# Rounding and splitting weights: gate and up halves made ahead of each product, down halves made once by the first block

## The chip, the cores and the metric

The kernel runs on one core of a Trainium2 chip. Five engines each work through an instruction stream of their own, strictly in order: TensorE (PE, matrix products), VectorE (DVE), ScalarE (ACT), GpSimd (POOL) and SyncE (SP, which here issues the transfers between DRAM and the on-chip memory). They wait for each other through semaphores. The metric is the time of one execution in device microseconds (us); lower is better.

## The reference

One layer of a hybrid decoder for 2048 prompt rows and 32 sample rows: a mixer (attention and a spatial gate) and then a SwiGLU block, all in float32. The change lies in the SwiGLU block and its weights alone:

```
D_MODEL = 1024
D_FF = 2816

def _swiglu(x, g, w_gate, w_up, w_down):
    h = _rmsnorm(x, g)
    return (jax.nn.silu(h @ w_gate) * (h @ w_up)) @ w_down

x = x + jnp.concatenate([att, u * gate], axis=-1) @ w_out
x = x + _swiglu(x, norm2_g, w_gate, w_up, w_down)
```

## The kernel before

**Precision.** PE multiplies rounded float32 values ("f32r"). To keep float32 accuracy every operand is split into a high part (the value rounded, made by a copy on ACT) and a low part (value minus high part, a subtraction on DVE or POOL). A product of two operands is then three matmuls: high by high, high by low and low by high. In `product` these are lines 1681, 1682 and 1683, and line 1683 is the one that reads the low part of the weights.

**Blocks and steps.** The SwiGLU block runs over three blocks of rows: the first and the second have six tiles of 128 rows, the third has four tiles and the sample rows. Each block runs over f = 0 to 21, the slices of 128 hidden columns. For one f the gate and up products are done with a scheme of seven products in place of eight (q = 0 to 6) on sums and differences of quarters of the weights; `one(u, q)` is one such step, and `product` issues its 12 matmuls (four values of k, three matmuls each). The outputs go to four PSUM banks in turn (`ps_m`), and after each product ACT or DVE takes them out (lines 1693 to 1719).

**Gate and up weights.** The first block loads the quarters (`load_quarter`), multiplies them with the norm's gain on ACT (`gained`, line 1575, four instructions of 128x128 for a quarter), forms the sums on POOL (`sums`, lines 1587 to 1596), stores the seven operands of each f to DRAM (`keep`, tensor `ab_d`), and splits them itself. The second and third block load the seven operands from `ab_d` (`load_source`, a ring of eight `fr` tiles) and split them: the high part by `high` (ACT, line 1603), the low part by `low_half` (POOL, line 1607), into a ring of five `op` tiles. `prepare` does this after the product of a step: behind product q of f it issues the low part of operand q + 3, the high part of operand q + 4 and the load of operand q + 4 of the next f.

**Down weights, first block.** `load_down` brings 128 rows of `w_down` for an even f into `rows2[1]` (tile `fe`) and for an odd f into `rows2[0]` (tile `fd`); `split_down` splits them (ACT line 136, POOL line 139, 128x1024) into tiles `dw`. The down products (`down_unit`, line 1961) follow steps 3, 4 and 5 of each even f, two tiles of rows each, in two PSUM banks (`ps_o`), and DVE adds each result to the row sums `acc` (line 1963). `block_sums` forms four differences of down weights for the later blocks on DVE (line 1652 at step 2 of an odd f, lines 1654 to 1656 at step 0 of the next even f) and stores them to `td_d` at step 4 of the odd f and step 2 of the even f.

**Down weights, second and third block.** Class `Seven` uses the seven-product scheme for the down products as well, on a pair of f (an odd f and the even one before it) and on pairs of row tiles. It needs seven weight operands d = 0 to 6 for a pair of f, an eighth (7) for the sample rows in the third block. Operands 2, 3, 4 and 6 come from `td_d`, operands 0, 1, 5 and 7 are halves of `w_down`; they are loaded at steps 1, 2 and 4 of the odd f (`load`), and `split` makes both parts (ACT line 1810; DVE or POOL line 1811) at steps 2 to 6 of the odd f and steps 0 and 2 of the even f. The hidden values get their own sums and splits (`even`, `odd_a`, `odd_b`, `odd_c`, `put`: lines 1815, 1816, 1850 to 1863). From step 3 of the even f on, `woven` puts one down product (three matmuls, line 1898) behind each k of the gate and up products until none is left: 21 for a pair in the second block; 14, and 4 of two matmuls for the sample rows, in the third. DVE adds each to `acc` (line 1900). Between step 1 of the odd f and step 2 of the even f there are no down products.

**Order.** Every engine's stream is in the order of the program text. `later(n, ...)` puts work n steps off, and `tick()`, called at the head of `one`, issues what is due. All these transfers go through SP, in order; SP waits where a tile isn't free or data isn't ready.

**Rings that matter here.** `zn_tile` gives one of three tiles of 128x512; in the first block an f uses two of them (the sums at steps 0 and 3). `rows2` are two single tiles. `roll` copies a piece of 512 KB of the caches in DRAM, once per f in the first block, three times in the second and twice in the third.

## Time and profile before

| | us |
|---|---|
| median of three runs | 2735.92 (2733.41 to 2742.21) |
| the profiled execution, its own time | 2734.9 |
| span of its instructions | 2733.1 |

| engine | busy us | share of the span | instructions |
|---|---|---|---|
| PE | 2496.4 | 91% | 13448 |
| DVE | 1772.7 | 65% | 3275 |
| POOL | 1457.0 | 53% | 1138 |
| ACT | 1286.2 | 47% | 2744 |

The SwiGLU block of the three row blocks lies at about 1017 to 1513 us, 1602 to 2139 us and 2216 to 2700 us of the span. In the views, a row of the timeline has the start in us, the duration in us, the engine, the line, the operation, output<-inputs, the shape, the count of instructions merged into the row, and in brackets how long the engine sat idle before it and what released it. A row of a group has the line, engine, operation, tiles, shapes and count, then busy us and mean ns of one, then idle time before it and its releasers. A row of a table by stretches has, for each engine, busy us and the number of instructions, then the granted PE clock (1.00 is full), the share of time in which the 16 DMA engines were busy, and GB/s.

### The profile page before, as it was taken

What the parts mean: (1) busy time and instruction counts of PE and PEld (TensorE: products, weight loads), DVE (VectorE), ACT (ScalarE), POOL (GpSimd) and SP (SyncE); (2) the same over time, 40 slices, a digit from 0 to 9 for tenths busy, and PEclk for the clock granted to TensorE, in tenths of its full rate; (3) what the DMA queues carried; (4) which work ended last, traced back from release to release, by engine and by line L of the source; (5) the groups of instructions that cost most, each with busy time, mean ns of one, the idle gap of its engine ahead of it and who ended that gap; (6) DMA issues with size and microseconds to landing.
All of it is one profiled execution on the core that took longest, in us unless ns stands there. A gap on an engine that the chain in (4) does not pass through costs nothing.

```text
span 2733.1 us, 39993 instructions
## 1 busy us (share of the span) xinstructions
PE 2496.4 (91%) x13448; PEld 2194.9 (80%) x13448; DVE 1772.7 (65%) x3275; ACT 1286.2 (47%) x2744; POOL 1457.0 (53%) x1138
## 2 busy tenths in 40 slices
PE   8998899999999889999999999999989998888886
PEld 6776777778888778999999888888878787777775
DVE  3268784438888775555555667777677756676666
ACT  5423344447777555545454463233342453333343
POOL 1035743234677457868686346455464445555553
PEclk9999999999999999999999999999999998898988
DMA  8764844677777655565655735555555645555553
GB/s 241 217 202 154 284 139 139 200 251 220 233 223 198 188 167 189 188 204 186 207 183 176 240 123 181 166 181 177 166 169 177 195 139 173 178 169 183 164 189 102
DMA packets 335307, 509.98 MB, mean 187 GB/s; under 512 B 28273, under 2 KB 181266, under 8 KB 329214
## 3 DMA queue, kind: packets, MB, share of 16 engines
q1 hardware_dynamic: 329628, 498.37, 57.8%
q10 hardware_dynamic: 5474, 9.04, 1.2%
q8 instruction: 108, 1.77, 0.3%
q14 instruction: 97, 0.79, 0.1%
HBM read 401.11 MB, written 176.32 MB: 211 GB/s over the span
## 4 chain that ended last, share of the span: by engine, by line
PE 32%; issue 11%; POOL 9%; DMA 5%; DVE 4%; ACT 2%; SPq 0%; POOLq 0%; ACTq 0%; DVEq 0%
POOL op L1607 7%; PE ps_m L1683 6%; PE ps_o L1961 6%; PE ps_m L1682 6%; PE ps_m L1681 6%; PE ps_o L1898 5%; DMA fd<-in_w_down_dram 3%; DMA fr<-ab_d 1%; DMA db<-td_d 1%; POOL db L1811 0%; DVE acc L1963 0%; POOL op L1811 0%; PE ps_o L1413 0%; PE ps_o L1415 0%; PE ps_o L1414 0%
## 5 line engine op out<-in xcount | busy, mean ns | idle before, releaser
L1683 PE MATMUL ps_m<-xh,op 128*128 128x384 f32 (+5 forms) x1932 | 638.8, 331 | 125.4 <-POOL op L1607 125.3
L1607 POOL TENSOR_TENSOR op<-fr,op 128x512 fp32r<-128x512 f32 x385 | 524.2, 1378 | 311.5 <-ACT op L1603 307.6
L1681 PE MATMUL ps_m<-xh,op 128*128 128x384 f32 (+5 forms) x1932 | 628.0, 325 | 0.3 <-DVE raw L1711 0.3
L1682 PE MATMUL ps_m<-xl,op 128*128 128x384 f32 (+5 forms) x1932 | 628.2, 325 | 0.0
L1683 PEld LDWEIGHTS ps_m<-xh,op 128*128 128x128 f32 x1932 | 381.8, 198 | 142.0 <-POOL op L1607 140.8
L1681 PEld LDWEIGHTS ps_m<-xh,op 128*128 128x128 f32 x1932 | 381.4, 197 | 21.5 <-issue 0.6
L1682 PEld LDWEIGHTS ps_m<-xl,op 128*128 128x128 f32 x1932 | 380.9, 197 | 17.8
L1900 DVE TENSOR_TENSOR acc<-acc,ps_o 128x512 f32<-128x512 f32 x350 | 239.7, 687 | 127.8 <-PE ps_o L1898 123.8
L1730 ACT ACTIVATE ps_t<-zn 128x384 f32<-128x384 f32 (+1 forms) x126 | 58.6, 465 | 507.6 <-DVE zn L1713 360.3
L1603 ACT ACTIVATE op<-fr 128x512 fp32r<-128x512 f32 x396 | 237.4, 619 | 43.9 <-PE ps_m L1683 37.0
L1961 PE MATMUL ps_o<-dw,hw 128*128 128x512 f32 x840 | 199.3, 392 | 5.5 <-DVE acc L1963 5.5
L319 PE MATMUL ps_s<-wh,xh 128*128 128x512 f32 x480 | 197.4, 411 | 7.3 <-ACT xh L136 6.1
L320 PE MATMUL ps_s<-wl,xh 128*128 128x512 f32 x480 | 191.4, 399 | 0.0
L321 PE MATMUL ps_s<-wh,xl 128*128 128x512 f32 x480 | 191.0, 398 | 0.0
L1961 PEld LDWEIGHTS ps_o<-dw,hw 128*128 128x128 f32 x840 | 156.6, 188 | 40.2 <-DVE acc L1963 8.8
L1963 DVE TENSOR_TENSOR acc<-acc,ps_o 128x512 f32<-128x512 f32 x142 | 96.7, 686 | 80.8 <-PE ps_o L1961 80.8
L1607 POOL TENSOR_TENSOR op<-pair,op 128x512 fp32r<-128x512 f32 x63 | 86.2, 1376 | 97.9 <-ACT op L1603 52.9
L1898 PE MATMUL ps_o<-op,ao 128*128 128x512 f32 x450 | 133.1, 406 | 0.0
L319 PEld LDWEIGHTS ps_s<-wh,xh 128*128 128x128 f32 x480 | 92.4, 192 | 37.1 <-issue 8.4
L321 PEld LDWEIGHTS ps_s<-wh,xl 128*128 128x128 f32 x480 | 92.3, 192 | 20.7 <-DVE xl L139 0.2
L320 PEld LDWEIGHTS ps_s<-wl,xh 128*128 128x128 f32 x480 | 92.8, 193 | 17.7 <-DVE wl L227 0.5
L612 POOL TENSOR_TENSOR vl<-kv,vh 100x512 fp32r<-100x512 f32 (+1 forms) x32 | 45.9, 1438 | 109.3 <-PE ps_t L622 37.0
(548 smaller groups left out, 5789.3 us busy)
## 6 DMA issues: line engine op xcount, KB each, us to landing
fr<-ab_d SPq DMA_DIRECT2D x308, 256.0 KB
out_ks_dram<-in_cache_k_dram SPq DMA_DIRECT2D x56, 512.0 KB
out_vs_dram<-in_cache_v_dram SPq DMA_DIRECT2D x56, 512.0 KB
ab_d<-fr SPq DMA_DIRECT2D x88, 256.0 KB
raw<-in_w_in_dram SPq DMA_DIRECT2D x72, 256.0 KB
fd<-in_w_down_dram SPq DMA_DIRECT2D x70, 256.0 KB
qk_d<-pair SPq DMA_DIRECT2D x64, 256.0 KB
ab_d<-pair SPq DMA_DIRECT2D x63, 256.0 KB
```

Of the source, the lines that this page charges most:

```text
L319: pe.matmul(o[j], xh[:, k, :], wh, start=(k == 0), stop=False)
L320: pe.matmul(o[j], xh[:, k, :], wl, start=False, stop=False)
L321: pe.matmul(o[j], xl[:, k, :], wh, start=False, stop=(k == KD - 1))
L1603: act.activation(ops[f, j][0], ab[f][j], AF.Copy)
L1607: (pool if f or j in POOL_LOW else dve).tensor_sub(lo_, ab[f][j], hi.bitcast(F32))
L1681: pe.matmul(out, wh[:, ks], xh[:, :, k], start=(k == 0), stop=False)
L1682: pe.matmul(out, wh[:, ks], xl[:, :, k], start=False, stop=False)
L1683: pe.matmul(out, wl[:, ks], xh[:, :, k], start=False, stop=(k == 3))
L1898: pe.matmul(ps, l_, r_, start=(new and x == 0), stop=(x == 2), skip_group_check=True)
L1900: dve.tensor_add(acc, acc, ps)
L1961: pe.matmul(ps[0:nr], l_, r_[:, cs], start=(z == 0 and y == 0), stop=(z == FC - 1 and y == len(pairs) - 1))
L1963: dve.tensor_add(B.acc[i][0:nr, cs], B.acc[i][0:nr, cs], ps[0:nr])
```

## The change

Two things change. **Gate and up weights:** in the second and third block, `one` now issues at its head, ahead of `tick()` and of product q, both the high and the low part of operand q + 4 (of operand q - 3 of the next f for q over 2) and the load that follows; `prepare` no longer does this after the product. **Down weights:** the first block now also makes the high part (`block_high`, ACT) and the low part (`block_low`, DVE, in place) of its four differences and stores both parts (`block_keep`, `td_d` is twice as large), and stores both parts of its split down weights (`down_keep`, new tensor `bd_d`). Its sums at step 0 of the even f move to step 5 of the odd f before; the steps of all this stand in the table `FIRST_DOWNS`, whose key is (f % 2, q). `load_down` of an even f moves from step 4 to step 3. In the second and third block `split`, `raw` and `source` are gone: `load` brings both parts of an operand with one transfer of 512 KB straight to where the products read it, operands 0 and 1 at step 1 of the odd f, 2 to 6 at steps 2 to 6, 7 at step 0 of the even f.

```diff
--- before.py
+++ after.py
@@ -118,7 +118,8 @@
     cs_d = dram.tile([SR, D], F32, name="cs_d")
     zs_d = dram.tile([3, SR, DA], F32, name="zs_d")
     ab_d = dram.tile([NF, 7, P, 512], F32, name="ab_d")
-    td_d = dram.tile([NF // 2 - 1, 4, P, 512], F32, name="td_d")
+    td_d = dram.tile([NF // 2 - 1, 4, P, 2, 512], F32, name="td_d")
+    bd_d = dram.tile([NF - 2, P, 2, D], F32, name="bd_d")
 
     ident = consts.tile([P, P], F32, name="ident")
     make_identity(nc, ident)
@@ -1645,20 +1646,54 @@
         raws["d", f] = w_ = rows2[0 if seven else 1 - f % FC]
         sync.dma_start(w_, A["w_down"][f * P:(f + 1) * P, :])
 
-    def block_sums(g, part):
+    def block_sum(g, first):
 
         (t1, t3), (t4, t2) = ((r_[:, 0:512], r_[:, 512:1024]) for r_ in (rows2[1], rows2[0]))
-        if part == 0:
+        if first:
             dve.tensor_sub(t1, t3, t1)
-        elif part == 1:
-            dve.tensor_sub(t3, t2, t3)
-            dve.tensor_sub(t2, t2, t1)
-            dve.tensor_sub(t4, t4, t2)
-        elif part == 2:
-            sync.dma_start(td_d[g, 0], t1)
-        else:
-            for j, t_ in ((1, t2), (2, t3), (3, t4)):
-                sync.dma_start(td_d[g, j], t_)
+            return
+        dve.tensor_sub(t3, t2, t3)
+        dve.tensor_sub(t2, t2, t1)
+        dve.tensor_sub(t4, t4, t2)
+
+    tops = {}
+
+    def block_high(j):
+        t_ = rows2[(1, 0, 1, 0)[j]]
+        src = t_[:, 0:512] if j in (0, 3) else t_[:, 512:1024]
+        hi = zn_tile()
+        act.activation(hi.bitcast(F32R), src, AF.Copy)
+        tops[j] = hi, src
+
+    def block_low(j):
+        hi, src = tops[j]
+        dve.tensor_sub(src.bitcast(F32R), src, hi)
+
+    def block_keep(g, j):
+        for z, x in enumerate(tops.pop(j)):
+            sync.dma_start(td_d[g, j, :, z], x)
+
+    def down_keep(f):
+        for z, x in enumerate(wd[f % FC]):
+            sync.dma_start(bd_d[f, :, z], x.bitcast(F32))
+
+    FIRST_DOWNS = {(1, 2): ((block_sum, True), (down_keep, -1)), (1, 3): ((block_high, 0),),
+                   (1, 5): ((block_sum, False), (block_low, 0)), (1, 6): ((block_keep, 0), (down_keep, 0), (block_high, 2)),
+                   (0, 0): ((block_low, 2),), (0, 1): ((block_keep, 2), (block_high, 1)), (0, 2): ((block_low, 1),),
+                   (0, 3): ((block_keep, 1), (block_high, 3)), (0, 4): ((block_low, 3),), (0, 5): ((block_keep, 3),)}
+
+    def first_downs_ahead(f, q):
+
+        g = f // 2 if f % 2 else f // 2 - 1
+        if not 0 <= g < NF // 2 - 1:
+            return
+        for fn, x in FIRST_DOWNS.get((f % 2, q), ()):
+            if fn is block_keep or fn is block_sum:
+                fn(g, x)
+            elif fn is down_keep:
+                fn(f + x)
+            else:
+                fn(x)
 
     wd = {}
 
@@ -1779,36 +1814,22 @@
             for key in ("s1", "s4"):
                 t_ = pair_tile().rearrange("p a b -> p (a b)")
                 self.a[key] = (self.flat(t_, 0), self.flat(t_, 384))
-            x = [op_tile(True) for _ in range(3)]
+            self.whole = [pool_["fg"].tile([P, 2, 512], F32R, name="op", tag="ox", bufs=3) for _ in range(3)]
             for _ in range(2):
                 t_ = ob_pair("db")
-                x += [(t_[z][:, 0:512], t_[z][:, 512:1024]) for z in range(2)]
+                self.whole += [x.rearrange("p (z c) -> p z c", z=2) for x in t_]
             if self.B.last:
-                x.append((self.B.spare[:, 0:512], self.B.spare[:, 512:1024]))
-            self.d = x
-
-        def source(self, g, d):
+                self.whole.append(self.B.spare.rearrange("p (z c) -> p z c", z=2))
+            self.d = [(x[:, 0], x[:, 1]) for x in self.whole]
+
+        def load(self, g, d):
             j = (None, None, 1, 0, 2, None, 3, None)[d]
             if j is not None:
-                return td_d[g, j]
-            f, half = {0: (0, 0), 1: (1, 0), 5: (1, 1), 7: (0, 1)}[d]
-            f += 2 * g
-            return A["w_down"][f * P:(f + 1) * P, half * 512:(half + 1) * 512]
-
-        def raw(self, d):
-            if d in (0, 1, 5, 7):
-                return rows2[0][:, 0:512] if d in (0, 5) else rows2[0][:, 512:1024]
-            return self.d[d][1].bitcast(F32)
-
-        def load(self, g, *ds):
-            for d in ds:
-                sync.dma_start(self.raw(d), self.source(g, d))
-
-        def split(self, eng, *ds):
-            for d in ds:
-                hi, lo_ = self.d[d]
-                act.activation(hi, self.raw(d), AF.Copy)
-                eng.tensor_sub(lo_, self.raw(d), hi.bitcast(F32))
+                src = td_d[g, j]
+            else:
+                f, half = {0: (0, 0), 1: (1, 0), 5: (1, 1), 7: (0, 1)}[d]
+                src = bd_d[2 * g + f][:, :, half * 512:(half + 1) * 512]
+            sync.dma_start(self.whole[d].bitcast(F32), src)
 
         def put(self, key, src, eng):
             hi, lo_ = self.a[key]
@@ -1930,16 +1951,11 @@
                     self.later_places()
                 if q in (2, 3):
                     self.even(q - 2)
-                if q in (1, 2, 4):
-                    self.load(g, *{1: (0, 1, 2, 3), 2: (4, 6), 4: (5, 7) if self.B.last else (5,)}[q])
-                for eng, ds in {2: ((dve, (0,)), (pool, (1,))), 3: ((dve, (2,)),), 4: ((pool, (3,)),),
-                                5: ((dve, (4,)),), 6: ((pool, (5,)),)}.get(q, ()):
-                    self.split(eng, *ds)
+                for d in ((), (0, 1), (2,), (3,), (4,), (5,), (6,))[q]:
+                    self.load(g, d)
             elif f % 2 == 0 and f:
-                if q == 0:
-                    self.split(pool, 6)
-                if q == 2 and self.B.last:
-                    self.split(pool, 7)
+                if q == 0 and self.B.last:
+                    self.load(g - 1, 7)
                 if f + 2 == NF and q == 3:
                     load_down(f)
 
@@ -2242,6 +2258,15 @@
 
         def one(u, q):
             f = u["f"]
+            if st and u["b"] == B.nt:
+                if f and q < 3:
+                    both_halves(f, q + 4)
+                    if f + 1 < NF:
+                        load_source(f + 1, q + 4)
+                if f + 1 < NF and q > 2:
+                    both_halves(f + 1, q - 3)
+                    if f + 2 < NF:
+                        load_source(f + 2, q - 3)
             tick()
             if st and f and f % 2 == 0 and q == 3:
                 st.begin(f // 2 - 1)
@@ -2253,12 +2278,7 @@
                     sources(B, 2, q, q + 1)
                 return
 
-            if st:
-                if f and q < 5:
-                    prepare(B, f, 4 + q)
-                if f + 1 < NF and q > 2:
-                    prepare(B, f + 1, q - 3)
-            else:
+            if not st:
                 if f and q < 2:
                     prepare(B, f, 7 + q)
                 if f + 1 < NF:
@@ -2283,20 +2303,17 @@
 
             if st and f + 2 < NF:
                 return
-            g = f // 2
             if f % 2 == 0:
-                if q == 4 and 0 < f and not st:
+                if q == 3 and 0 < f and not st:
+                    first_downs_ahead(f, q)
                     load_down(f)
                 if q == 6:
                     split_down(f)
                     load_down(f + 1)
-                if q in (0, 2) and 0 < f and not st:
-                    block_sums(g - 1, 1 + q)
-            else:
-                if q == 3:
-                    split_down(f)
-                if q in (2, 4) and f + 1 < NF and not st:
-                    block_sums(g, q - 2)
+            elif q == 3:
+                split_down(f)
+            if not st and (f % 2 or q != 3):
+                first_downs_ahead(f, q)
 
         def downs_of(pair, a, b):
             for i in rows[a:b]:
```

## The prediction

> **What bounds the kernel now.** I read the groups of the page first, then stretches of the span, then the timeline of PE around one pair of f in each block. PE is busy for 91% of the span, so a gain has to come from its idle time. One group holds nearly all of that in the SwiGLU blocks: the third matmul of a step, the one that needs the low part of a gate or up weight, has waited 125.3 us for POOL's subtraction. In the table by stretches the first block (first row) has PE busy without a gap at full clock, though DVE, ACT and POOL have 44, 50 and 27% of their time free; the second and third block (next two rows) have PE idle and the clock at 0.98 and 0.88. The last row is one stretch without down products in the third block.
>
> ```profile
> span 2733.1 us, 39993 instructions
> ...
> L1683 PE MATMUL ps_m<-xh,op 128*128 128x384 f32 (+5 forms) x1932 | 638.8, 331 | 125.4 <-POOL op L1607 125.3
> ```
>
> ```profile
> core 0: us, PE busy (x) PEld busy (x) DVE busy (x) ACT busy (x) POOL busy (x), PEclk, DMA share, GB/s
> 1097.00:1507.00 410.00, 410.00 (x2158) 383.61 (x2157) 228.09 (x342) 204.68 (x506) 299.18 (x214) 1.00 0.58 190
> 1645.00:2085.00 440.00, 404.00 (x2033) 366.81 (x2034) 313.08 (x491) 148.97 (x296) 230.96 (x167) 0.98 0.53 172
> 2257.00:2660.00 403.00, 333.04 (x1943) 305.29 (x1942) 269.48 (x524) 153.00 (x349) 232.09 (x180) 0.88 0.54 175
> 2418.40:2437.20 18.80, 14.64 (x99) 14.43 (x98) 10.82 (x25) 9.24 (x22) 10.60 (x8) 0.82 0.71 238
> ```
>
> How much is it in all? The wait costs its idle time, and the matmuls behind it run at a lower clock. Both are in the length of a pair of f. The timeline of PE gives it from the same wait at step 2 of f = 2 and, nine pairs later, of f = 20; the other rows are starts of steps of k where nothing waits.
>
> ```profile
> 1645.55 0.69 PE L1683 MATMUL ps_m<-xh,op 128*128 128x384 f32 x1 [2.08 <-POOL op L1607]
> ...
> 2095.95 0.65 PE L1683 MATMUL ps_m<-xh,op 128*128 128x384 f32 x1 [2.59 <-POOL op L1607]
> ...
> 2260.72 0.59 PE L1683 MATMUL ps_m<-xh,op 128*128 128x272 f32 x1 [3.54 <-POOL op L1607]
> ...
> 2666.09 0.60 PE L1683 MATMUL ps_m<-xh,op 128*128 128x272 f32 x1 [3.22 <-POOL op L1607]
> ```
>
> ```profile
> 1653.80 0.34 PE L1681 MATMUL ps_m<-xh,op 128*128 128x384 f32 x1
> ...
> 1656.25 0.34 PE L1681 MATMUL ps_m<-xh,op 128*128 128x384 f32 x1
> ...
> 1678.56 0.33 PE L1681 MATMUL ps_m<-xh,op 128*128 128x384 f32 x1
> ...
> 1680.64 0.33 PE L1681 MATMUL ps_m<-xh,op 128*128 128x384 f32 x1
> ...
> 2403.62 0.29 PE L1681 MATMUL ps_m<-xh,op 128*128 128x272 f32 x1
> ...
> 2407.90 0.29 PE L1681 MATMUL ps_m<-xh,op 128*128 128x272 f32 x1
> ...
> 2419.96 0.29 PE L1681 MATMUL ps_m<-xh,op 128*128 128x272 f32 x1
> ...
> 2424.49 0.29 PE L1681 MATMUL ps_m<-xh,op 128*128 128x272 f32 x1
> ```
>
> Second block: a pair takes (2095.95 - 1645.55) / 9 = 50.0 us. Its 56 steps of k would take, without a wait, 21 with a down product at (1656.25 - 1653.80) / 2 = 1.22 and 35 bare ones at (1680.64 - 1678.56) / 4 = 0.52: 43.9 us. Third block: a pair takes 405.37 / 9 = 45.0 us; 14 steps with a down product at (2407.90 - 2403.62) / 4 = 1.07, 38 bare ones at (2424.49 - 2419.96) / 12 = 0.38, and 4 with two sample matmuls, put at 0.38 + 2/3 of 0.69 = 0.84, make 32.7 us. The excess is 6.1 and 12.3 us per pair.
>
> Why POOL is late is seen on ACT, at the same place in every pair: ACT stands before the high part of a down weight until its transfer has landed, the high parts of the gate and up weights queue behind it, and POOL, which then has both kinds of subtraction to do, starts 4.39 us late.
>
> ```profile
> 2423.98 0.63 ACT L1810 ACTIVATE op<-fd 128x512 fp32r<-128x512 f32 x1 [1.10 <-DMA fd<-in_w_down_dram]
> 2425.64 0.63 ACT L1810 ACTIVATE op<-fd 128x512 fp32r<-128x512 f32 x1 [1.02 <-DMA fd<-in_w_down_dram]
> 2426.17 0.61 ACT L1603 ACTIVATE op<-fr 128x512 fp32r<-128x512 f32 x1
> ```
>
> ```profile
> 2426.34 1.26 POOL L1811 TENSOR_TENSOR op<-fd,op 128x512 fp32r<-128x512 f32 x1 [4.39 <-ACT op L1810]
> ```
>
> **Second and third block: what goes.** All `split` work goes: per pair seven or eight ACT copies with their waits for transfers, three DVE and four or five POOL subtractions. The groups of the third block (2257 to 2660 us of the span) price POOL; the last row is a split of a hidden sum, which stays and is used under the rivals.
>
> ```profile
> L1607 POOL TENSOR_TENSOR op<-fr,op 128x512 fp32r<-128x512 f32 x126 | 168.5, 1355 | 98.4 <-ACT op L1603 98.4
> ...
> L1811 POOL TENSOR_TENSOR db<-db 128x512 fp32r<-128x512 f32 x18 | 24.6, 1364 | 0.0
> ...
> L1811 POOL TENSOR_TENSOR op<-fd,op 128x512 fp32r<-128x512 f32 x9 | 11.4, 1266 | 43.3 <-ACT op L1810 43.3
> ...
> L1816 DVE TENSOR_TENSOR pair<-fe,pair 128x256 fp32r<-128x256 f32 x9 | 13.5, 1496 | 0.0
> ```
>
> From step 1 of the odd f to step 2 of the even f there are nine bare products, 9 x 1.51 = 13.6 us in the third block. POOL has nine low parts there, 9 x 1.36 = 12.2 us, and before the change four or five of the others, about 6 us: 18 us for 13.6, and so a wait. Without them it fits. The ring of five `op` tiles lets operand q + 5 be rounded once product q has ended; 0.61 + 1.36 = 2.0 us later it is ready, and it is needed four products (6.0 us) after. ACT still stands at the SiLU and at the hidden values' splits, 2 to 3 us each, inside that lead. Issuing both halves ahead of the product, rather than the low part a step later, adds lead that the tile ring mostly takes away again; I give it nothing of its own.
>
> I therefore take the whole excess for 9.5 pairs (f = 1 to 19 and half of the last pair, whose own down weights are split as before): 9.5 x (6.1 + 12.3) = 175 us.
>
> **What comes in: transfers.** Each down operand doubles to 512 KB. In the third block the bare stretch then asks for nine loads of 0.26 MB, eight of 0.52 MB and three cache pieces of 0.52 MB, 8.1 MB. The bare stretch of the table moved 238 GB/s at a DMA share of 0.71, so about 335 GB/s is full: 24 us for 13.6. Up to operand 6 (step 6 of the odd f) 6.3 MB are ahead, 19 us; it is needed after the stretch, step 3 (4.3 us) and 2.5 us of step 4, 20.4 us from the start. That is just in time; between 0 and 4 us late per pair I take 1.5, nearer the lower end because the rate above is from a stretch with the same mix. Ten pairs: 15 us. The second block has a stretch of 19.4 us, 27 us until operand 6, and 6.8 MB (20 us) ahead of it: nothing. Left is 175 - 15 = 160 us.
>
> **First block: what it pays.** PE has no gap there, so nothing can be won, and every wait is new. Per pair: four ACT copies (0.61 each), four DVE subtractions, three of the sums moved from the even f's step 0 to the odd f's step 5, and 3 MB of stores more. Averaged, all fits in the free time. The order does not. These rows show the place where it is tight, f = 9 to 10 (step 5 of the odd f ends at 1237.5, step 2 of the even f at 1245.6):
>
> ```profile
> 1237.50 0.55 DVE L1713 TENSOR_TENSOR zn<-zn,ps_m 128x384 f32<-128x384 f32 x1 [0.94 <-PE ps_m L1683]
> ...
> 1240.17 0.57 DVE L1738 TENSOR_TENSOR ps_t<-ps_t,raw 128x384 f32<-128x384 f32 x1
> ...
> 1242.82 1.50 DVE L1654 TENSOR_TENSOR fe<-fd,fe 128x512 f32<-128x512 f32 x1
> 1244.42 1.62 DVE L1655 TENSOR_TENSOR fd<-fd,fe 128x512 f32<-128x512 f32 x1
> 1246.07 0.69 DVE L1656 TENSOR_TENSOR fd<-fd 128x512 f32<-128x512 f32 x1
> ...
> 1247.90 0.55 DVE L1707 TENSOR_TENSOR zn<-raw,ps_m 128x384 f32<-128x384 f32 x1
> 1249.29 0.69 DVE L1963 TENSOR_TENSOR acc<-acc,ps_o 128x512 f32<-128x512 f32 x1 [0.84 <-PE ps_o L1961]
> ```
>
> ```profile
> 1241.38 0.84 ACT L1742 ACTIVATE hw<-ps_t 128x384 fp32r<-128x384 f32 x2
> ...
> 1243.09 2.44 ACT L1575 ACTIVATE fr<-fr,g2c 128x128 f32<-128x128 f32 x8
> 1245.44 0.47 ACT L1693 ACTIVATE zn<-ps_m 128x384 f32<-128x384 f32 x1
> ```
>
> ```profile
> 1237.62 2.41 POOL L139 TENSOR_TENSOR dw<-fd,dw 128x1024 fp32r<-128x1024 f32 x1
> ```
>
> ```profile
> 1247.70 5.64 PE L1961 MATMUL ps_o<-dw,hw 128*128 128x512 f32 x24
> ```
>
> DVE's four subtractions of two on-chip operands take 0.69 to 1.6 us, the more the busier POOL is. After the change DVE starts the three sums at 1238.05; the second writes where POOL's split still reads until 1240.03, so it ends near 1241.7, the third at 1243, `block_low(0)` at 1244.6. Queued behind on DVE are the hidden values of step 6 (lines 1738, 1719, 1738: three times 0.57, until 1246.3, before the change 1240.7). For them wait ACT's two copies of line 1742, and behind those on ACT one high part, the eight gains (2.44 us), `block_high(2)` and the taking out of the even f's product 0 (line 1693): near 1250.7, was 1245.9. Behind it on DVE come `block_low(2)`, lines 1695 and 1697, `block_low(1)` and line 1707, which ends near 1254 (was 1248.45). Only then can DVE add the first down product. PE begins these at 1247.7 and has two banks of six matmuls, 5.64 / 24 x 6 = 1.4 us each, so from about 1250.5 it waits until 1254.7: 4.3 us. SP, too, stands at `block_keep(0)` until 1244.6, and behind it the loads of the next quarters, which ACT wants at step 3 and, itself late, just about gets. Line 1707 also needs a `zn` tile that `block_high(2)` used and that is stored by then, behind some 2.75 MB on SP's queue: at 335 GB/s from 1246 on that is 1254.5, landing a little later. I put the wait at 5.5 us, and 2 us for the lower clock after it, as in the third block, where a pair loses 12.3 us. Bounds: 1 us if POOL leaves DVE alone (four at 0.69), 11 if both the stores and the sums are slow. Ten pairs: 75 us, 10 to 110.
>
> **Sum.** 2734.9 (this execution's own time; 1.0 under the median) - 160 + 75 = 2650 us.
>
> The clock has a rule against part of this. In the second block waits of 2.08 and 2.59 us come with a clock of 0.98. The Trainium skill, page "TensorE: Matmul & The Clock Gate", section "HAM oscillation — how this bites in real kernels", gives "no PE-idle gaps >~3.4µs" as the rule; by it those waits would cost no clock, and their removal would win some 19 us less there (estimate of mine, by that page). The measured 0.98 decides against it here.
>
> **Rivals.** (a) The first block hides its new work: POOL idles in it for 27% of the time, DVE's sums start 5 us earlier, the lead of PE's operands is long. Against: DVE's line 1707 had 1.3 us to spare and gets three subtractions and an ACT queue ahead. Then 2734.9 - 160 + 0 to 20, about 2585. (b) Half of the gain is eaten where POOL no longer waits: DVE's splits of the hidden sums, up to 1.5 us each, have three bare products (4.5 us) without the wait that gave them time, or operand 6 lands late. For: DVE is busy for 67% of the third block (269 of 403 us). Against: the sums are wanted only by the down products of step 3, one k after the other. With a quarter to a half eaten, 2734.9 - 120 + 75 = 2690 to 2734.9 - 80 + 75 = 2730. (c) Slower: the stores in the first block. The `zn` tile of `block_high(2)` comes free only when its store lands, behind 3 MB; at the 190 GB/s that this block moves on average, and not 335, that is 16 us, landing at 1262 to 1264, and DVE and then PE stand until then. It decides from 16 us per pair, where it equals the 160; at 20 us the time is 2734.9 - 160 + 200 = 2775. Against it: 190 goes with a share of 0.58. (d) No change: the low parts are as late as before for a cause that I do not see, and the first block hides its part: 2735.
>
> **How the numbers follow.** Forecast 0.62, (a) 0.16, (b) 0.11, (c) 0.08, (d) 0.03. Predicted is the forecast's 2650. The forecast's own bounds are 2734.9 - 160 + 10 = 2585 and, with operand 6 late by 3 us a pair, 2734.9 - 145 + 110 = 2700. The range 2575 to 2715 holds these, (a) and the better part of (b). A run of this kernel can tell 0.3% (8 us) from no change. Faster holds the forecast, (a) and nearly all of (b): 0.88; slower is (c): 0.08; the same: 0.04.
>
> **What would show it.** In the second and third block no line 1810 or 1811, the wait of line 1683 for POOL under 20 us, pairs of 44 and 33 to 35 us, clock near 1.00. In the first block a new wait of line 1961 for DVE's line 1963 of 4 to 7 us in each even f, pairs of 53 us in place of 45.7, and dips of the clock. I am wrong if the first block stays without gaps, if pairs of the third stay over 38 us, or if PE there waits for DVE or a transfer.

## The result, and where the time went

The changed kernel takes 2663.8 us (median of 4 runs, 2657.6 to 2667.0) against 2738.1 for the kernel before on the same chips (4 runs, 2733.4 to 2742.2): a ratio of 0.973, 95% interval 0.970 to 0.975. Its profiled execution took 2664.5 us, with a span of 2662.4.

Rows of the page of the changed kernel; the first matmul of a step is now line 1716, the third, which waited 125.3 us for POOL before, is line 1718, the down product of the first block is line 1977, and the woven one of the other two blocks is line 1919.

```profile
span 2662.4 us, 39857 instructions
...
L1716 PE MATMUL ps_m<-xh,op 128*128 128x384 f32 (+5 forms) x1932 | 612.7, 317 | 13.2 <-ACT hw L1777 12.9
L1718 PE MATMUL ps_m<-xh,op 128*128 128x384 f32 (+5 forms) x1932 | 612.1, 317 | 2.8 <-POOL op L1608 2.8
...
L1977 PE MATMUL ps_o<-dw,hw 128*128 128x512 f32 x840 | 219.9, 417 | 36.2 <-DVE acc L1979 36.2
...
L1919 PE MATMUL ps_o<-op,ao 128*128 128x512 f32 x450 | 130.6, 400 | 26.5 <-ACT ps_t L1765 26.5
```

The old wait is gone, and two others have grown: 36.2 us of line 1977, of which 32.2 lie in the first block (5.5 us before the change, 1.5 of it there), and 26.5 us of the woven down products, which waited 0.5 us before. What each block takes is seen in the table by stretches, from the first to the last product of each block. After the change:

```profile
1020.02:1585.30 565.28, 517.86 (x2664) 474.65 (x2662) 330.49 (x467) 275.82 (x663) 377.82 (x263) 0.96 0.64 222
1673.94:2162.54 488.60, 478.99 (x2574) 444.86 (x2573) 347.33 (x578) 161.38 (x309) 228.41 (x166) 1.00 0.65 223
2243.17:2629.72 386.55, 365.51 (x2444) 337.44 (x2443) 284.08 (x614) 148.78 (x350) 211.44 (x163) 0.99 0.71 262
```

And the same stretches of the kernel before:

```profile
1017.09:1513.38 496.29, 492.42 (x2664) 462.07 (x2663) 277.11 (x427) 254.41 (x623) 366.89 (x263) 1.00 0.57 189
1602.01:2138.84 536.83, 493.82 (x2574) 452.31 (x2573) 376.30 (x608) 192.03 (x381) 286.60 (x206) 0.98 0.52 169
2216.49:2700.55 484.06, 403.17 (x2444) 372.13 (x2442) 319.45 (x644) 188.06 (x430) 276.58 (x213) 0.89 0.51 166
```

The first number behind the stretch is its length, the second PE's busy time; the difference is PE's idle time, and a change of the busy time of the same count of matmuls is put down to the clock, whose mean stands in the third number from the end.

| block | before | after | change | of it idle | of it clock |
|---|---|---|---|---|---|
| first | 496.3 | 565.3 | +69.0 | +43.6 | +25.4 |
| second | 536.8 | 488.6 | -48.2 | -33.4 | -14.8 |
| third | 484.1 | 386.6 | -97.5 | -59.8 | -37.7 |

The sum is -76.7; the span fell by 70.7. The other 6 us lie ahead of the first block (its first product starts 2.9 us later) and between the second and the third (3.0 us). Ahead of the first block nothing was changed, and over the runs here the start moved between 1013.1 and 1021.6 us, and the stretch between the second and the third block between 77.4 and 80.6 us; both are scatter.

### The profile page after: what moved, and what is told of

Its sections match the earlier page's. It is cut to its first block, busy times and chain, and to the rows that moved or that the text cites. A ratio compares the mean times of both kernels' runs of the same rounds, so it can differ in the third digit from the quotient of the medians.

```text
span 2662.4 us, 39857 instructions
## 1 busy us (share of the span) xinstructions
PE 2472.7 (93%) x13448; PEld 2166.2 (81%) x13448; DVE 1763.9 (66%) x3255; ACT 1237.9 (46%) x2634; POOL 1345.7 (51%) x1048
## 3 DMA queue, kind: packets, MB, share of 16 engines
q8 instruction: 108, 1.77, 0.3%
## 5 line engine op out<-in xcount | busy, mean ns | idle before, releaser
L1716 PE MATMUL ps_m<-xh,op 128*128 128x384 f32 (+5 forms) x1932 | 612.7, 317 | 13.2 <-ACT hw L1777 12.9
L1718 PE MATMUL ps_m<-xh,op 128*128 128x384 f32 (+5 forms) x1932 | 612.1, 317 | 2.8 <-POOL op L1608 2.8
L1717 PE MATMUL ps_m<-xl,op 128*128 128x384 f32 (+5 forms) x1932 | 611.6, 317 | 0.0
L1716 PEld LDWEIGHTS ps_m<-xh,op 128*128 128x128 f32 x1932 | 365.3, 189 | 37.5 <-ACT hw L1777 15.8
L1717 PEld LDWEIGHTS ps_m<-xl,op 128*128 128x128 f32 x1932 | 365.1, 189 | 18.1
L1718 PEld LDWEIGHTS ps_m<-xh,op 128*128 128x128 f32 x1932 | 364.9, 189 | 3.3 <-POOL op L1608 3.3
L1604 ACT ACTIVATE op<-fr 128x512 fp32r<-128x512 f32 x396 | 243.0, 622 | 165.2 <-PE ps_m L1718 93.8
L1977 PE MATMUL ps_o<-dw,hw 128*128 128x512 f32 x840 | 219.9, 417 | 36.2 <-DVE acc L1979 36.2
L1977 PEld LDWEIGHTS ps_o<-dw,hw 128*128 128x128 f32 x840 | 166.5, 201 | 80.3 <-DVE acc L1979 45.4
L1919 PE MATMUL ps_o<-op,ao 128*128 128x512 f32 x450 | 130.6, 400 | 26.5 <-ACT ps_t L1765 26.5
L320 PEld LDWEIGHTS ps_s<-wh,xh 128*128 128x128 f32 x480 | 93.0, 194 | 36.2 <-issue 8.4
L1919 PEld LDWEIGHTS ps_o<-op,ao 128*128 128x128 f32 x450 | 79.6, 189 | 38.3 <-ACT ps_t L1765 31.3
```

What stands on the lines that cost most here:

```text
L320: pe.matmul(o[j], xh[:, k, :], wh, start=(k == 0), stop=False)
L1604: act.activation(ops[f, j][0], ab[f][j], AF.Copy)
L1716: pe.matmul(out, wh[:, ks], xh[:, :, k], start=(k == 0), stop=False)
L1717: pe.matmul(out, wh[:, ks], xl[:, :, k], start=False, stop=False)
L1718: pe.matmul(out, wl[:, ks], xh[:, :, k], start=False, stop=(k == 3))
L1919: pe.matmul(ps, l_, r_, start=(new and x == 0), stop=(x == 2), skip_group_check=True)
```

## What stands behind the two new waits

**First block.** PE's rows of the down products in f = 10 of the changed kernel:

```profile
1278.18 2.92 PE L1977 MATMUL ps_o<-dw,hw 128*128 128x512 f32 x12
1284.26 5.49 PE L1977 MATMUL ps_o<-dw,hw 128*128 128x512 f32 x12 [3.16 <-DVE acc L1979]
```

Twelve matmuls fill two banks, then PE waits 3.16 us for DVE's add of the first; the next twelve take 5.49 us where the twelve before took 2.92. DVE's timeline at the same place:

```profile
1266.75 0.55 DVE L1748 TENSOR_TENSOR zn<-zn,ps_m 128x384 f32<-128x384 f32 x1 [0.94 <-PE ps_m L1718]
1267.22 2.60 DVE L1655 TENSOR_TENSOR fe<-fd,fe 128x512 f32<-128x512 f32 x1
1269.92 1.61 DVE L1656 TENSOR_TENSOR fd<-fd,fe 128x512 f32<-128x512 f32 x1
1271.56 1.67 DVE L1657 TENSOR_TENSOR fd<-fd 128x512 f32<-128x512 f32 x1
1273.15 1.77 DVE L1670 TENSOR_TENSOR fe<-fe,zn 128x512 fp32r<-128x512 f32 x1
...
1276.36 1.21 DVE L1326 TENSOR_TENSOR hw<-ps_t,hw 128x384 fp32r<-128x384 f32 x2
1280.38 0.69 DVE L1670 TENSOR_TENSOR fe<-fe,zn 128x512 fp32r<-128x512 f32 x1 [2.82 <-ACT zn L1665]
...
1283.07 0.54 DVE L1742 TENSOR_TENSOR zn<-raw,ps_m 128x384 f32<-128x384 f32 x1
1283.53 0.67 DVE L1979 TENSOR_TENSOR acc<-acc,ps_o 128x512 f32<-128x512 f32 x1
```

And ACT's:

```profile
1277.39 2.44 ACT L1576 ACTIVATE fr<-fr,g2c 128x128 f32<-128x128 f32 x8
1279.73 0.61 ACT L1665 ACTIVATE zn<-fe 128x512 fp32r<-128x512 f32 x1
1280.25 0.47 ACT L1728 ACTIVATE zn<-ps_m 128x384 f32<-128x384 f32 x1
```

Two things are added to DVE's queue: the sums (lines 1655 to 1657) with the first subtraction, 7.7 us at the end of the odd f, and a subtraction (line 1670 at 1280.38) that stands 2.82 us for its copy, because ACT makes that copy late (line 1665, behind the gains). The evacuations, and behind them the adds that free the banks, wait in the same queue. Which of the two counts is what the experiments had to tell.

**Third block.** DVE, then PE, in step 3 of f = 14:

```profile
2491.02 1.34 DVE L1884 TENSOR_TENSOR zn<-zn,fe 128x256 f32<-128x256 f32 x1
2492.28 0.96 DVE L1837 TENSOR_TENSOR pair<-fe,pair 128x256 fp32r<-128x256 f32 x1
...
2494.94 1.47 DVE L1921 TENSOR_TENSOR acc<-acc,ps_o 128x512 f32<-128x512 f32 x2
```

```profile
2492.86 0.86 PE L1919 MATMUL ps_o<-op,ao 128*128 128x512 f32 x3
2495.71 0.93 PE L1919 MATMUL ps_o<-op,ao 128*128 128x512 f32 x3 [1.61 <-ACT ps_t L1765]
```

The third woven product starts a new sum in a bank that an earlier one still holds; DVE takes it out from 2494.94 on, after its work on the hidden sums, and PE goes on at 2495.71. The row names ACT's line 1765 as what ended the wait; by the times it is DVE's add of line 1921: in all 20 such waits of the second and third block PE starts 0.10 us after the end of such an add, but 0.17 us after the end of ACT's instruction in the one block and 0.27 us in the other.

## The experiments

Times are medians; runs with one time say so. Where no other kernel is named, the edit is made to the changed kernel. The kernel before took 2742.1 to 2745.4 us beside the runs with an edit, and their ratios are to those times. The last columns are the three blocks, first product to last product.

| run | us | first | second | third |
|---|---|---|---|---|
| before | 2738.1 | 496.3 | 536.8 | 484.1 |
| after | 2663.8 | 565.3 | 488.6 | 386.6 |
| order alone (one time) | 2740.8 | 496.3 | 547.9 | 476.2 |
| old order (one time) | 2651.5 | 565.4 | 479.4 | 389.0 |
| no down stores (one time) | 2652.0 | 567.1 | 488.5 | 380.9 |
| wet steps | 2595.5 | 498.4 | 488.6 | 389.8 |
| begin later | 2643.4 | 565.5 | 477.2 | 378.3 |
| all in the even unit | 2667.7 | 572.0 | 488.6 | 387.9 |
| the same, sums stay (one time) | 2695.0 | 603.2 | 488.6 | 385.8 |
| the same, old order, begin later | 2647.5 | 571.7 | 478.9 | 380.2 |
| wet steps, own tile | 2594.4 | 500.2 | 488.5 | 387.1 |
| wet steps, own tile, begin later | 2574.2 | 498.4 | 477.3 | 379.2 |
| wet steps, own tile, sums stay (one time) | 2620.7 | 528.0 | 488.5 | 387.2 |
| order alone, begin later (one time) | 2685.4 | 496.3 | 523.6 | 442.6 |

**The order alone**, made to the kernel before:

```diff
+            if st and u["b"] == B.nt:
+                if f and q < 3:
+                    both_halves(f, q + 4)
...
             tick()
...
-            if st:
-                if f and q < 5:
-                    prepare(B, f, 4 + q)
...
```

> The kernel before with the first half of the change alone: both parts of a gate or up operand are issued ahead of the product, the down weights are split in the second and third block as before. Theory (the down weights' splits hold ACT and POOL): the wait of the third matmul of a step for POOL stays above 80 us (125 before), the first block's stage stays at 496 us, the time falls by 0 to 30 us, to about 2720. Rival (the lead is what helps): the wait falls below 30 us and the time to about 2590, since the first block then pays nothing.

Measured: 2740.8 us, no change. The page of this run (product lines 1681 and 1683, woven product 1898):

```profile
L1681 PE MATMUL ps_m<-xh,op 128*128 128x384 f32 (+5 forms) x1932 | 624.6, 323 | 35.3 <-DVE raw L1711 35.3
...
L1683 PE MATMUL ps_m<-xh,op 128*128 128x384 f32 (+5 forms) x1932 | 623.3, 323 | 2.8 <-POOL op L1607 2.8
...
L1898 PE MATMUL ps_o<-op,ao 128*128 128x512 f32 x450 | 142.6, 429 | 86.6 <-DVE acc L1900 86.6
```

This was not foreseen: the wait for POOL goes from 125.3 to 2.8 us by the order alone, and waits for DVE of 86.6 and 35.3 us take its place. Neither side had it: the theory has the time right and the wait wrong, the rival the wait right and the time wrong. In the kernel before, DVE was close behind POOL: it had 0.35 us to spare at 1951.75, ahead of its first add of the woven products of f = 14 in the second block, in steps in which PE had just stood three times for POOL, 5.0 us in all.

**The old order** (the reverse: down weights loaded split, operands prepared behind the product as before):

```diff
-            if st and u["b"] == B.nt:
-                if f and q < 3:
-                    both_halves(f, q + 4)
...
+            if st:
+                if f and q < 5:
+                    prepare(B, f, 4 + q)
...
```

> The changed kernel without the first half of the change: down weights split once by the first block, gate and up operands prepared behind the product as before. Theory: time within 10 us of the changed kernel's 2664; the third matmul of a step waits for POOL for under 20 us (2.8 after, 125 before). Rival (the lead is what helps): the wait comes back, 60 us or more, and the time is 2720 or more.

Measured: 2651.5 us, and 6.2 us of wait for POOL. Loading the weights split removes the waits for POOL and most of those for DVE, with either order; here the new order costs 9.2 us in the second block, where line 1919 waits 0.3 us without it and 9.1 with it, and wins 2.4 in the third. There line 1919 waits 8.5 us for transfers of down weights with the old order, against 1.8 with the new.

**No down stores.** Operands 0, 1, 5 and 7 are other numbers here:

```diff
-    FIRST_DOWNS = {(1, 2): ((block_sum, True), (down_keep, -1)), (1, 3): ((block_high, 0),),
+    FIRST_DOWNS = {(1, 2): ((block_sum, True),), (1, 3): ((block_high, 0),),
...
-                src = bd_d[2 * g + f][:, :, half * 512:(half + 1) * 512]
+                src = td_d[g, 2 * f + half]
```

> The changed kernel without the stores of both parts of the split down weights by the first block (2 MB less per pair of f); the later blocks load operands 0, 1, 5 and 7 from the stored sums instead, with transfers of the same size, so their down products are of other numbers. Theory (the first block waits for DVE and ACT, by the order of their work): the pairs of f in the first block stay at 51 to 53 us (52.9 after, 45.7 before), the time at 2650 to 2666. Rival (the stores delay the tile of the high part): pairs fall below 48 us and the time below 2620.

Measured: the first block keeps its length (567.1) without 20 MB of its stores. The third block is 5.7 us faster; its loads come from `td_d` alone there, and PE waits for none of them. Whether that is the whole reason is not shown: the waits that went were 1.8 us.

**Wet steps.** The first block's new work is moved to the steps in which down products run (called wet here) or just before:

```diff
-                   (1, 5): ((block_sum, False), (block_low, 0)), (1, 6): ((block_keep, 0), (down_keep, 0), (block_high, 2)),
-                   (0, 0): ((block_low, 2),), (0, 1): ((block_keep, 2), (block_high, 1)), (0, 2): ((block_low, 1),),
-                   (0, 3): ((block_keep, 1), (block_high, 3)), (0, 4): ((block_low, 3),), (0, 5): ((block_keep, 3),)}
+                   (1, 4): ((block_low, 0),), (1, 5): ((block_keep, 0),), (1, 6): ((down_keep, 0),),
+                   (0, 0): ((block_sum, False),),
+                   (0, 3): ((block_high, 2),), (0, 4): ((block_low, 2), (block_high, 1)),
+                   (0, 5): ((block_keep, 2), (block_low, 1), (block_high, 3)), (0, 6): ((block_keep, 1), (block_low, 3), (block_keep, 3))}
```

The even f's `load_down` moves to step 5. `block_low(0)` overwrites its difference before the sums use it, so that two of the four differences are other numbers; the instructions and transfers are the same.

> The changed kernel with the first block's new work at other steps: the three sums back at step 0 of the even f, the copies and subtractions of differences 1 to 3 and their stores at steps 3 to 6 of the even f, where down products run and DVE and ACT have time; load_down of the even f at step 5. The same instructions and stores. Theory: the first block's pairs fall from 52.9 us to 45.7 to 46.5, the waits of the down products for DVE to under 8 us in all (36 after), the time to about 2600 (2592 to 2612). Rival (the amount of work or of stores, not its place): pairs stay above 50 us, the time at 2640 or more.

Measured: 2595.5 us, ratio to before 0.945 (0.941 to 0.948), and the first block is back at 498.4 with every copy, subtraction and store still in it.

**Begin later**, in the second and third block:

```diff
-            if st and f and f % 2 == 0 and q == 3:
+            if st and f and f % 2 == 0 and q == 4:
                 st.begin(f // 2 - 1)
```

> The changed kernel, with the woven down work of a pair begun one step later (fifth product of the even step instead of the fourth), nothing else. Theory: what is left in blocks 2 and 3 is the wait of the woven product for its PSUM bank (26.5 us at line 1919, 0.85 us per pair in the second block, 1.62 in the third), because VectorE's add into that bank stands behind the hidden sums of the same even step; one step later VectorE has caught up. Expected: that wait under 5 us, first block 565 as after, second block 476 to 482 instead of 488.6, third block 365 to 378 instead of 386.6, time 2630 to 2645 against 2663.8. Rival (late transfers of the down weights set the third block): the later begin leaves fewer steps and more transfers in flight at the end of a pair, third block 385 to 395, time 2650 to 2668.

Measured: 2643.4 us, the second block as expected, the third at the edge of it; the wait of line 1919 falls from 26.5 to 6.2 us, a little more than the 5 given. PE's wait is therefore DVE's lateness in that step; the late transfers of the rival are no limit, PE waits for none here. Not all of it went: in the third block the sample rows' products (line 1927) now wait 8.9 us for DVE's adds.

**All in the even unit**, where the sums find their difference whole (with `load_down` at step 5):

```diff
+    FIRST_DOWNS = {(1, 2): ((block_sum, True), (down_keep, -1)), (1, 6): ((down_keep, 0),),
+                   (0, 0): ((block_sum, False),), (0, 2): ((block_high, 0),),
+                   (0, 3): ((block_low, 0), (block_high, 2)), (0, 4): ((block_keep, 0), (block_low, 2), (block_high, 1)),
+                   (0, 5): ((block_keep, 2), (block_low, 1), (block_high, 3)), (0, 6): ((block_keep, 1), (block_low, 3), (block_keep, 3))}
```

> The changed kernel, with the first block's sums and differences of the down weights moved from steps 6, 7 of the odd and 1 to 6 of the even unit to step 1 (sums) and steps 3 to 7 (differences, each low part one step behind its high part) of the even unit; the same operations and stores, and the even unit's down weights loaded at its step 6 instead of 4. Theory: the 3.2 us waits of line 1977 are VectorE's three sums (5.9 us) in the last steps of the odd unit, which make the hidden values, then ScalarE's copies, then VectorE's evacuations late; without them there the first block takes 497 to 503 us instead of 565.3, blocks 2 and 3 as after, time 2594 to 2605. Rival (the work itself, or its 20 MB of stores, costs what it costs wherever it stands): first block 540 to 567, time 2638 to 2666.

Measured: 2667.7 us, the first block at 572.0; the theory, that the sums alone were late, fell. The rival's ranges (540 to 567, 2638 to 2666) are just missed too, and its reason, the work itself, is refuted by the run with the wet steps, which has the same work. What is late instead is seen in f = 14 of this run, on DVE, ACT and PE:

```profile
1388.77 0.56 DVE L1742 TENSOR_TENSOR zn<-raw,ps_m 128x384 f32<-128x384 f32 x1
1393.95 1.78 DVE L1670 TENSOR_TENSOR fe<-fe,zn 128x512 fp32r<-128x512 f32 x1 [4.63 <-ACT zn L1665]
```

```profile
1392.77 0.63 ACT L1604 ACTIVATE op<-pair 128x512 fp32r<-128x512 f32 x1 [3.51 <-POOL pair L1594]
1393.31 0.61 ACT L1665 ACTIVATE zn<-fe 128x512 fp32r<-128x512 f32 x1
```

```profile
1396.39 1.22 PE L1977 MATMUL ps_o<-dw,hw 128*128 128x512 f32 x2 [4.89 <-DVE acc L1979]
```

DVE has nothing to do for 4.63 us: the subtraction of step 3 stands at the head of its queue, its copy of step 2 stands on ACT behind the rounding of a sum that POOL has not made yet (3.51 us), and the adds that PE wants are behind the subtraction.

**The same, with the sums left in step 5 of the odd f:**

```diff
-                   (0, 0): ((block_sum, False),), (0, 2): ((block_high, 0),),
+                   (1, 5): ((block_sum, False),), (0, 2): ((block_high, 0),),
```

> As the one with sums and differences moved, but the three sums stay in step 6 of the odd unit; only the splits of the differences and their stores are moved. Theory (the sums start the chain of late work): the first block keeps most of its loss, 540 to 565 us, time 2638 to 2664. Rival (VectorE standing for ScalarE's copies of the differences, in steps 1 to 3 of the even unit, is what delays the adds): first block 497 to 512, time 2594 to 2612.

Measured: 2695.0 us, the first block at 603.2: longer than either theory gave, and 31.2 us longer than with the sums moved. The sums do cost.

**All in the even unit, old order, begin later:** the edits of these three runs in one kernel.

> Three edits together: sums and differences of the first block moved as above, the operand splits of blocks 2 and 3 issued behind the product of their step as in the kernel before, and the woven down work begun one step later. Theory (the three act in different blocks or on different waits): first block 497 to 503, second 472 to 480, third 370 to 384, time 2565 to 2588. Rival (the late begin and the old order answer the same wait, and late transfers take what they free): second block 476 to 480, third 388 to 395, time 2585 to 2600.

Measured: 2647.5 us. The first block failed as above; the second and the third (478.9 and 380.2) are those of the later begin with the new order (477.2 and 378.3). Once the woven work begins later, the order is worth 2 us at most in either block.

**Wet steps, own tile.** The schedule of the wet steps, with a tile of its own for the first low part:

```diff
         hi, src = tops[j]
-        dve.tensor_sub(src.bitcast(F32R), src, hi)
+        lo_ = src if j else zn_tile()
+        dve.tensor_sub(lo_.bitcast(F32R), src, hi)
+        tops[j] = hi, lo_
```

> The changed kernel with the first block's sums at step 1 of the even unit, difference 1 copied, subtracted and stored at steps 4 to 6 of the odd unit (its low part in a tile of its own, so that the sums still find it whole), differences 2 to 4 copied from step 4 of the even unit on, each subtracted a step later. Theory (what costs is a subtraction in VectorE's queue whose copy on ScalarE is still to come, ahead of the adds that the down products wait for; where a step with down products of 5.5 us lies between copy and subtraction it is free): first block 497 to 503 us, no wait of the down products over 0.5 us, time 2594 to 2604. Rival (the zn ring of three, one of which now holds the low part, makes the evacuations wait in the odd unit): first block 510 to 530, time 2608 to 2630. Rival 2 (the work costs wherever it stands): 560, 2660.

Measured: 2594.4 us, ratio to before 0.946 (0.945 to 0.947), the first block at 500.2. The waits of the down product (line 1980 here) are down from 36.2 us to 7.0, of which 3.0 lie in the first block. Two of these waits, of 2.0 and 0.7 us at f = 2, are over the 0.5 that was expected:

```profile
L1980 PE MATMUL ps_o<-dw,hw 128*128 128x512 f32 x840 | 201.7, 395 | 7.0 <-DVE acc L1982 7.0
```

**The same, with the sums put back** in step 5 of the odd f:

```diff
-                   (1, 4): ((block_low, 0),), (1, 5): ((block_keep, 0),), (1, 6): ((down_keep, 0),),
-                   (0, 0): ((block_sum, False),),
+                   (1, 4): ((block_low, 0),), (1, 5): ((block_sum, False), (block_keep, 0)), (1, 6): ((down_keep, 0),),
```

> The schedule that brought the first block back to 500 us, with one thing put back where the change had it: the three sums of the down weights in step 6 of the odd unit instead of step 1 of the even one. Theory (only a subtraction that stands in VectorE's queue before its copy is made costs much; the sums are work that finds room): first block 497 to 515 us, waits of the down products under 1.2 us per pair, time 2594 to 2612. Rival (the sums' 5.9 us start the chain of late work by themselves): first block 525 to 565, time 2620 to 2660.

Measured: 528.0 us in the first block, 2620.7 in all: the rival's range, at its lower edge. DVE and PE in step 4 of f = 12:

```profile
1321.52 0.69 DVE L1671 TENSOR_TENSOR fe<-fe,zn 128x512 fp32r<-128x512 f32 x1 [1.27 <-ACT zn L1665]
1322.13 1.28 DVE L1981 TENSOR_TENSOR acc<-acc,ps_o 128x512 f32<-128x512 f32 x2
```

```profile
1322.87 3.01 PE L1979 MATMUL ps_o<-dw,hw 128*128 128x512 f32 x12 [1.03 <-DVE acc L1981]
```

So neither cause is alone. With the differences placed well, the sums' place costs 528.0 - 500.2 = 27.8 us; with the sums where the change has them, the differences' place (with their stores, the tile and the step of `load_down`, which moved along) costs 565.3 - 528.0 = 37.3. Together that is the 65 us between 500.2 and 565.3. In this run PE waits twice in each pair: 1.4 us after step 3, where DVE's evacuation stands for an ACT copy that is late behind the gains and no subtraction is in the way, and 1.0 us after step 4, behind the subtraction shown. So the sums at the end of the odd f make ACT's copies late, and a subtraction that stands for such a copy adds to it.

**Both cures together**, the edits of the wet steps with the own tile and of the later begin:

> The same with the woven down work of a pair begun one step later in blocks 2 and 3. Theory (the two act in different blocks, so their gains add: 20.5 us of the later begin, 565 - 499 = 66 us of the first block): 2663.8 - 20.5 - 66 = 2577, between 2572 and 2586. Rival (they share a limit, the down weights' loads or the clock): 2588 to 2600.

Measured: 2574.2 us (2573.8 to 2580.2), ratio to before 0.939 (0.938 to 0.941): the gains add, and this version beats both kernels. Its three blocks in the table by stretches:

```profile
1016.64:1515.00 498.36, 494.66 (x2664) 463.12 (x2663) 306.14 (x468) 275.45 (x663) 370.79 (x263) 1.00 0.72 251
1603.65:2080.90 477.25, 476.75 (x2574) 445.23 (x2572) 345.91 (x578) 160.31 (x309) 228.18 (x166) 1.00 0.66 228
2159.90:2539.13 379.23, 363.31 (x2444) 334.33 (x2443) 282.53 (x614) 148.87 (x350) 210.13 (x163) 1.00 0.72 267
```

In the second block PE is idle for 0.5 us of 477.

**The order alone with the later begin**, these two edits made to the kernel before:

> The kernel before with only the new order of the operand splits (both halves ahead of the product) and the woven down work begun one step later; the down weights are still loaded whole and split in blocks 2 and 3. Theory (VectorE's work on the down weights, of which loading them split relieves it, is what the adds of the woven products stand behind; a later begin moves that wait and does not end it): second block 515 to 545 us, third 450 to 476, time 2700 to 2738. Rival (where the woven work begins was the limit, and loading the weights split was not needed): second block 476 to 485, third 380 to 400, time 2570 to 2610, since its first block keeps 496.

Measured: 2685.4 us, better than the theory allowed and far from the rival's 2570 to 2610. The two small moves win 54.7 us of the second and third block (1020.9 to 966.2) with no transfer changed; that the weights come split wins another 110.7 (to 855.5 in the run with the later begin). The later begin without the new order was not run on the kernel before. What is left in this run is DVE:

```profile
L1898 PE MATMUL ps_o<-op,ao 128*128 128x512 f32 x450 | 135.4, 412 | 58.3 <-DVE acc L1900 57.8
```

## Why the prediction was right, step by step

The forecast was 2650 in a range of 2575 to 2715; the time is 2663.8. Its two large terms have the right sign and nearly the right size. Their causes are right in the main, since the splits were what PE waited for and the order of DVE's queue is what the first block pays; what was left out is DVE's own lateness in the second and third block.

- **Second block, 9.5 x 6.1 = 58 us: measured 48.2.** A pair takes 45.3 us (first products of f = 4 and f = 18: 317.25 / 7) where 43.9 were worked out. The difference is the woven product's wait, 0.85 us a pair (9.1 us in the block), and what hangs on it: with the later begin the pair takes 44.2, with the old order too. The weak step is the sentence that gives the order of the operand splits "nothing of its own": in the second block it costs 9.2 us unless the woven work is begun later.
- **Third block, 9.5 x 12.3 less 15 for transfers = 102: measured 97.5.** The total is right, its second part is not. PE's and its weight loads' idle time before the woven product, by its line in this block:

```profile
  ACT ps_t L1765: 36.7, 20
...
  DMA db<-td_d: 1.3, 2
  DMA db<-bd_d: 0.5, 1
```

  PE waited 1.8 us for late transfers (8.5 in the run with the old order), not 15. The rate of 335 GB/s was too low a limit: the stretch 2277.0 to 2286.2 quoted in the last section moved 403. In their place stands rival (b)'s mechanism, DVE's work on the hidden sums, but at 1.6 to 2.4 us a pair, 17.4 in all for PE itself (the 36.7 counts its weight loads as well), and not a quarter to a half of the gain; the later begin gave 8.3 us back here and 11.4 in the second block. The two make 19.2 us, the 9.5 x 12.3 = 117 less 97.5 that was measured: that a term of 15 for transfers came near it is luck.
- **The cause.** The prediction took POOL's lateness for the whole of it. POOL's wait did fall under 20 us (2.8). But the order alone ends it too and wins nothing: DVE is late then, 4.8 us a pair in the second block, where POOL had cost 4.2. So the gain needed DVE to be relieved as well. The prediction counted DVE's three subtractions a pair and gave them no share. How much of DVE's relief is those three, and how much the splits on ACT and POOL that it no longer waits for or runs beside, no run separates.
- **First block, 5.5 + 2.0 us a pair, 75 in all: measured 4.4 + 2.5, 69.0.** The chain stands row by row. With the end of step 5 as zero (line 1713 at 1237.50 before, line 1748 at 1266.75 after: 29.25 us apart) the prediction's line 1707, "near 1254", is line 1742's end at 1283.61 - 29.25 = 1254.4. The down products began 1.2 us later than put (1278.18 - 29.25 = 1248.9), since PE itself had waited 0.96 us ahead of step 3 (12.9 us of line 1716 in the page, 4.3 of it at f = 2, a wait that was not foreseen), so the wait was 3.16 and not 4.3. The addition of 1.2 us for a `zn` tile behind the stores did not come: line 1742 starts without a gap in the DVE rows above, and with 20 MB fewer stores the block keeps its length.
- **The rivals.** (a), a first block that hides its work at 2585, is false of this change, but true of the work: placed otherwise it fits, at 2594.4. (b) is true in kind and small in size, as said. (c), the stores, is refuted by the same run, which keeps them all, and by the one without 20 MB of them. (d) is false.

The marks named ahead came out so: pairs of 45.3 (44 given) and 35.2 (first products of f = 4 and 18, 246.27 / 7; 33 to 35 given), a clock of 1.00 and 0.99, and pairs of 52.8 (f = 6 to 18, 316.96 / 6; 53 given) in the first block. The wait there is 3.2 us in nearly every even f, where 4 to 7 was given. One of the signs of being wrong came true in small: PE in the third block does wait for DVE and for transfers, by the 19.2 us above.

## What to carry to other kernels

An engine that is half idle can still set the pace by the order of its queue: before work is added to it, ask what stands behind each new instruction and whether its input is made by then, on a queue that may itself be waiting for a third engine. Put copy and subtraction on different sides of a long stretch of matmuls, and let work begin a step later where the engine that must empty its banks is busiest. A wait that one engine's name stands beside may hide a second engine only a little less late; take the first away alone, and see, as the run of the order alone did here.

## What the runs showed of the hardware

**The clock after a gap.** After the gap of 1.61 us shown above, three matmuls took 0.93 us against 0.86 ahead of it; after one of 2.41 us they took 1.33 and 1.48. PE in step 3 of f = 2 of the third block, and two stretches with such gaps, of 2.41 and of 1.61 us (the clock is the third number from the end):

```profile
2279.47 0.86 PE L1919 MATMUL ps_o<-op,ao 128*128 128x512 f32 x3
2283.12 1.33 PE L1919 MATMUL ps_o<-op,ao 128*128 128x512 f32 x3 [2.41 <-ACT ps_t L1765]
2284.94 1.48 PE L1919 MATMUL ps_o<-db,pair 128*128 128x512 f32 x3
```

```profile
2277.00:2286.20 9.20, 6.79 (x34) 5.82 (x33) 7.40 (x12) 3.99 (x10) 5.89 (x5) 0.85 1.03 403
2313.50:2319.70 6.20, 4.59 (x30) 4.08 (x30) 6.09 (x10) 2.94 (x7) 4.51 (x5) 1.00 1.02 400
```

The Trainium skill, page "TensorE: Matmul & The Clock Gate", section "HAM oscillation — how this bites in real kernels", asks for no gap over about 3.4 us; here 2.41 and 3.16 us already cost clock, and the measurement decides.

The length of a gap alone does not settle it below that. In the 14 traces, from the first product of the first block to the last of the third, the granted clock fell to half during the gap or within 1 us after it for all 68 gaps of PE over 3.41 us, 61 of 85 between 2.5 and 3.41, 10 of 31 between 1.9 and 2.5, and 8 of 114 between 1.3 and 1.9. In these blocks such a stretch of half clock lasted 3.41 us or a whole multiple of it.

**DVE beside POOL.** The same subtraction of line 1670 took 1.77 us at 1273.15 and 0.69 at 1280.38, where POOL was idle. In this trace the 15 of them with no POOL instruction beside them took 0.68 to 0.70 us, the other 25 took 0.69 to 1.78. POOL in the first of these stretches:

```profile
1266.87 2.41 POOL L140 TENSOR_TENSOR dw<-fd,dw 128x1024 fp32r<-128x1024 f32 x1
1269.22 1.75 POOL L1608 TENSOR_TENSOR op<-fr,op 128x512 fp32r<-128x512 f32 x1
1270.94 1.73 POOL L1597 TENSOR_TENSOR pair<-fr,pair 128x512 f32<-128x512 f32 x1
1272.63 1.74 POOL L1608 TENSOR_TENSOR op<-pair,op 128x512 fp32r<-128x512 f32 x1
```

The ends alternate: POOL's at 1269.28, 1270.97, 1272.67 and 1274.37, DVE's at 1269.82, 1271.53, 1273.23 and 1274.92, each engine ending an instruction some 1.7 us after its own last one. The alternation fits the Trainium skill, page "SBUF — State Buffer", section "SBUF: two separate sides", by which the ports that the two share are held by one instruction at a time. The 1.7 us are less than the 0.69 and 1.29 that the two take alone (POOL's at 1277.57), one after the other, so some part of each overlaps; no run here took POOL's work away to show the cause.
